# One more pair of FFN tiles by seven products, one pair fewer in the split by token halves

## The chip, the cores and the metric

The kernel runs on one core of a Trainium2 chip. The metric is the device time of one launch in microseconds, as the median of several runs. The engines are TensorE (PE in the profile, with its weight loads as PEld), VectorE (DVE), ScalarE (ACT), GpSimd (POOL) and SyncE (SP, which issues the DMAs). TensorE's clock has two levels, 1.2 and 2.4 GHz; the profile gives the granted clock as a share of the higher.

## The reference, cut to what matters

Two layers (DEPTH = 2) of a hybrid diffusion backbone work on 128 context tokens and 512 latent tokens, D = 1024, FFN width 2816. What the change touches is the FFN of each layer:

```
h = _rmsnorm(x, g_pre_ffn[l]) * (1.0 + sc2) + sh2
y = (jax.nn.silu(h @ w_ffn_gate[l]) * (h @ w_ffn_up[l])) @ w_ffn_down[l]
x = x + gt2 * _rmsnorm(y, g_post_ffn[l])
```

Behind it the next layer begins with a norm and modulation of x and its input projection; after layer 1, x is the output.

## The kernel before, in words

All 640 tokens are worked together, features on the partitions. The tokens lie in two halves of 320 columns (HW): half 0 holds the 128 context tokens and 192 latent ones, half 1 the rest. The input h is eight tiles `hk[k]`, one for 128 features each. Every fp32 operand is split into a high and a low fp32r part, and a product is three passes (high x high, high x low, low x high). A matmul in the profile has 320 columns; one weight tile of 128 output features over all 1024 inputs and one token half takes 8 x 3 = 24 of them.

**The FFN.** Its 22 feature tiles are worked in six groups (`GROUPS` = 4, 3, 3, 4, 4, 4). For each tile there is a pair of weight tiles, gate and up. A group first makes `acts` (silu of gate times up, split again in two parts), and then adds its share of the down projection w_dn to `z`, eight output tiles for each half (`dn`, `ev_dn`).

**Two ways for a pair.** The plain way, `ev_ffn`, runs gate and up for one half: 48 matmuls. The other, `seven`, makes both halves of a pair at once from seven products of half the depth, 7 x 12 = 84 matmuls. It reads sums of h made beforehand (tiles `th`; a sum also takes the place of half 1 of `hk[0..3]`) and sums of the weight tiles, made when the weights are split (a job of kind "sums"; a job "second" splits only the second half of a tile, to `hu`), and needs seven additions on VectorE.

**The last group** has four pairs. Two go by `seven` (`early = gn - 2`). Then the pool for weights is closed and opened anew as stage "c", the lane `second_block` turns half 1 of `hk[0..3]` back into h (tile `tb`), and the other two pairs go by halves: for half 0 gate and up of both pairs, then w_dn for half 0; then, after the flag ("block", l), the same for half 1. When half 0's z is complete, the lane `boundary` carries it on beside half 1's matmuls: the norm over features (`norm_scale`: two matmuls `nps` from the sums of squares `ssqz`, then `rsqrt` on ScalarE and VectorE), eight steps `post` (gated norm plus residual `xl`), in layer 0 a second norm and eight steps `pre` and `modulate`, which write half 0 of the next layer's `hk` (a high part, then a low part). The next layer's first products read half 0. In layer 1 `boundary` only writes the output y. Half 1 goes the same way afterwards.

**What sets the order.** Every engine works its instructions in the order in which they are written out. `drive` writes them: a main generator, `bulk`, gives TensorE's products, lanes such as `boundary` and `second_block` put their steps in between by a clock of estimated costs (`Clock`), and a stream of weights feeds the splits. `vg` and `copy` choose VectorE, POOL or ScalarE by the same clock. Weights come by SP's DMAs into a ring of three raw tiles, in the fixed order of `items`; a split frees its raw tile, and goes to the outer ring (three tiles `hl`, place 0) or to the stage's own pool (place 1). The list `jobs` holds kind, place and stage of every split. The edit stands in the loop that fills `items` and `jobs` (lines 576 to 596), and in the last group (lines 2054 to 2097).

Of the kernel before, what the change touches and what calls it, by code (L numbers as in the profile page):

```python
# [335 lines left out]
def emit(ctx, tc, a, o):  # L336
# [101 lines left out]
    def until(flag):  # L438
        while flag not in flags:
            yield WAIT  # L440

    def room(n):
        while live[0] + n > NSLOT:
            yield WAIT
# [114 lines left out]
    def plain(src, k, n, where, when):  # L559
        items.append((src, k, n))  # L560
        jobs.append(("plain", (len(items) - 1,), 1, where, when))

    for l in range(DEPTH):
        for c, u in [(c, u) for c in ((0, 1, 2) if l == 0 else (0, 2, 1)) + (3, 4, 5, 6, 7) for u in range(2)] + [(9, 0), (8, 0), (8, 1), (9, 1), (10, 0), (10, 1)]:
            k, n = (4, 256) if c in VCH else (KT, 128)
            plain(a["win"][l, c, u].rearrange("p (k n) -> p k n", n=n), k, n, int(l > 0 and (1 <= c <= 2 or (c == 3 and u == 1))), "c")
        for c in range(8):
            plain(a["wout"][l, c], KT, 128, int(c >= 3), "a")
        kb, turns = 0, 0

        def place():
            nonlocal turns
            turns += 1
            return (turns - 1) // 3 % 2

        for gi, gn in enumerate(GROUPS):
            last = gi == len(GROUPS) - 1
            for k in range(gn):
                gu = [(a["wgu"][l, 2 * (kb + k) + i], KT, 128) for i in range(2)]
                if gi and k < gn - 2 * last:  # L580

                    items.extend(gu)
                    g, u = len(items) - 2, len(items) - 1
                    jobs.append(("plain", (g,), 0, place(), "b"))
                    jobs.append(("second", (u,), 0, 2, "b"))
                    jobs.append(("sums", (g, u), 1, place(), "b"))
                    jobs.append(("plain", (u,), 1, place(), "b"))
                else:
                    for i in range(2):
                        plain(*gu[i], int(k == gn - 1) if last else int(2 * k + i >= 3), "c" if last else "a")  # L590
            t = a["wdn"].tensor
            for m in range(0, 8, 2):
                off = l * DFF * D + 128 * kb * D + m * 128 * gn * 128
                src = bass.AP(t, off, [[gn * 128, 128], [128 * gn * 128, 2], [1, gn * 128]])
                plain(src, 2 * gn, 128, int(m < 6) if last else place(), "c" if last else "b")
            kb += gn

    class Stream:
# [93 lines left out]
    stream = Stream()  # L692
# [786 lines left out]
    def bulk():  # L1479
# [117 lines left out]
        for l in range(DEPTH):  # L1597
# [183 lines left out]
            hls = [(nm, m, stream.next()) for nm, m in (("ag", 1), ("rg", 0), ("rg", 1))]  # L1781
# [68 lines left out]
            hls = [stream.next() for _ in range(2)]  # L1850
# [160 lines left out]
            for gi, gn in enumerate(GROUPS):  # L2011
                first_, last = gi == 0, gi == len(GROUPS) - 1
# [25 lines left out]
                if first_:  # L2038

                    hls = []  # L2040
                    for half in range(2):
                        for k in range(gn):
                            if half == 0:
                                hls.append((stream.next(), stream.next()))
                            ps = yield from mm_multi([(hl, half) for hl in hls[k]], hk, hk2key)
                            ev_act(silu(ps[0]), ps[1], acts[k], half)
                            if half:
                                stream.done(*hls[k])
                    flags.add(("first", l))
                    hpool("b", 3)  # L2050
                    mods_in[0] = True
                    yield from room(3)
                    z4 = [u5([128, 2, TOK], "z") for _ in range(3)]
                    zt = lambda k, z4=z4: z4[k // 2][:, k % 2, :]
                else:
                    yield from until(("sums", l))
                    early = gn - 2 if last else gn
                    for k in range(early):
                        yield from seven(acts[k])
                if last:  # L2060
                    if l == 0:
                        yield from until("mods1")
                    hpool("c", 5)
                    free(6)
                    yield from room(2)
                    spawn(second_block(), True)
                    sz = u5([128, 4, HW], "ssqz")
                    ssqs = [[sz[:, i], sz[:, 2 + i]] for i in range(2)]

                    hls = [(stream.next(), stream.next()) for _ in range(2)]  # L2070
                    hds = []
                    for half in range(2):
                        if half:
                            yield from until(("block", l))
                        for k in range(2):
                            yield from ev_ffn(*hls[k], acts[early + k], half)
                            if half:
                                stream.done(*hls[k])
                        if half:
                            lnexp()  # L2080
                        for i in range(4):
                            if not half:
                                hds.append(stream.next())
                            jobs = [(hds[i], 2 * i + m, half) for m in range(2)]
                            if i == 0:
                                yield from dn(jobs)
                            else:
                                for job in jobs:
                                    yield from dn([job])
                            if half:  # L2090
                                stream.done(hds[i])
                        if half == 0:
                            xls = yield from residual(0, xsrc)
                            spawn(boundary(0, zt, ssqs[0], xls, dst, nxt, der[l][:, 3]))
                else:
                    for i in range(4):
                        if len(z4) == i:
                            yield from room(1)
                            z4.append(u5([128, 2, TOK], "z"))
                        hl = stream.next()  # L2100
                        jobs = [(hl, 2 * i + m, half) for m in range(2) for half in range(2)]
                        if i == 0:
                            yield from dn(jobs)
                        else:
                            for job in jobs:
                                yield from dn([job])
                        stream.done(hl)
# [137 lines left out]
```

## Time and profile before

| what | us |
|---|---|
| median of 3 runs (1647.58 to 1650.80) | 1648.89 |
| the profiled execution's own time | 1650.12 |
| its span, first to last instruction | 1648.3 |
| TensorE busy in it | 1591.3 (97%) |
| VectorE busy in it | 1175.3 (71%) |
| ScalarE busy in it | 737.2 (45%) |

The span is what the rows below are timed in, from its start. A row of the timeline is a run of like instructions on one engine; the number in square brackets is the time in which the engine stood idle before it, and behind the arrow what ended that. Every instruction has the line of one helper, so that rows are told apart by their tiles: `acc<-h` are products with h (gate and up, or the next layer's projections), `acc<-act` are w_dn, `nps<-ssqz` is the norm's sum, `hl<-raw` a weight split.

### The profile page before, as it was taken

The numbers are of one execution on the slowest core, as the hardware profiler recorded it, in microseconds if no ns is written. First come the engines' busy times: TensorE is split into PE (matmuls) and PEld (weight loads), VectorE is DVE, ScalarE is ACT, GpSimd is POOL, SyncE is SP. The second block draws the span as 40 slices with busy tenths as digits, with TensorE's granted clock in tenths as the row PEclk, the third lists the DMA queues.
The fourth block names the chain that finished last, engine by engine and source line by source line (L and its number), as shares of the span: only waits on it lengthen the run. The fifth ranks groups of instructions, "written<-read, shape, count | busy, mean of one in ns | idle before, by whom it ended". The sixth has DMA issues, their size and how long they took to land.

```text
span 1648.3 us, 31142 instructions
## 1 busy us (share of the span) xinstructions
PE 1591.3 (97%) x12400; PEld 1479.7 (90%) x12400; DVE 1175.3 (71%) x2346; ACT 737.2 (45%) x1531; POOL 288.7 (18%) x331
## 2 busy tenths in 40 slices
PE   5998999999999999999999999899999999999997
PEld 3887888999999989999999978788999999999996
DVE  6388866758767667676696589777686677767666
ACT  5345654756322323242364466647653333334232
POOL 0101142023100001010143021341231010101012
PEclk9999999999999999999999999899999999999998
DMA  9431332352455655232342211113331213132222
GB/s 379 144 128 51 112 112 72 118 174 96 154 191 184 217 200 183 75 103 65 122 137 90 81 45 55 62 43 121 117 119 60 84 52 105 57 109 93 74 84 96
DMA packets 80002, 188.16 MB, mean 114 GB/s; under 512 B 7633, under 2 KB 38257, under 8 KB 79857
## 3 DMA queue, kind: packets, MB, share of 16 engines
q1 hardware_dynamic: 79856, 186.17, 33.2%
q8 instruction: 98, 1.61, 0.4%
q14 instruction: 48, 0.39, 0.1%
HBM read 173.42 MB, written 12.71 MB: 113 GB/s over the span
## 4 chain that ended last, share of the span: by engine, by line
PE 75%; DVE 13%; ACT 4%; issue 3%; DMA 3%; POOL 1%; SPq 0%; DVEq 0%; POOLq 0%; ACTq 0%
PE acc L235 57%; PE acct L235 6%; PE mps L235 3%; DVE hl L235 2%; DVE gE L235 1%; DMA mraw<-in_wmod 1%; PE rops L235 1%; DVE z L235 1%; DVE qbd L235 1%; DVE sg L235 1%; PE nps L235 1%; DMA raw<-in_wgu 1%; PE nsp L235 1%; DVE raw L235 1%; ACT hl L235 1%
## 5 line engine op out<-in xcount | busy, mean ns | idle before, releaser
L235 PE MATMUL acc<-h,hl 128*128 128x320 f32 x4800 | 758.2, 313 | 5.7 <-DVE h L235 2.0
L235 PEld LDWEIGHTS acc<-h,hl 128*128 128x128 f32 x4800 | 711.2, 188 | 28.7 <-issue 14.9
L235 DVE TENSOR_TENSOR hl<-raw,hl 128x1024 fp32r<-128x1024 f32 (+1 forms) x219 | 264.2, 1213 | 84.6 <-ACT hl L235 84.1
L235 PE MATMUL acc<-act,hl 128*128 128x320 f32 x2112 | 316.7, 310 | 2.2 <-DVE z L235 1.0
L235 PEld LDWEIGHTS acc<-act,hl 128*128 128x128 f32 x2112 | 310.4, 188 | 7.8 <-issue 3.3
L235 ACT ACTIVATE hl<-raw 128x1024 fp32r<-128x1024 f32 (+1 forms) x204 | 206.5, 1034 | 184.3 <-DVE raw L235 93.2
L235 POOL TENSOR_TENSOR raw<-raw 128x512 f32<-128x512 f32 x45 | 59.7, 1327 | 520.6 <-DVE hu L235 469.3
L235 PE MATMUL acct<-hl,h 128*128 128x256 f32 x960 | 137.4, 294 | 2.8 <-DVE hl L235 2.4
L235 PEld LDWEIGHTS acct<-hl,h 128*128 128x128 f32 x960 | 122.2, 193 | 11.4 <-issue 5.9
L235 PE MATMUL acc<-th,hl 128*128 128x320 f32 x768 | 120.0, 310 | 1.3 <-DVE hl L235 0.7
L235 PEld LDWEIGHTS acc<-th,hl 128*128 128x128 f32 x768 | 113.9, 188 | 5.1 <-issue 2.5
L235 ACT ACTIVATE act<-sg 128x320 fp32r<-128x320 f32 x64 | 30.2, 472 | 160.2 <-DVE sg L235 160.2
L235 DVE TENSOR_TENSOR z<-z,acc 128x320 f32<-128x320 f32 x160 | 72.5, 480 | 26.5 <-PE acc L235 26.1
L235 DVE TENSOR_TENSOR act<-sg,act 128x320 fp32r<-128x320 f32 x88 | 50.2, 571 | 35.2 <-ACT act L235 34.4
L235 DVE TENSOR_TENSOR raw<-raw 128x512 f32<-128x512 f32 x83 | 57.2, 689 | 21.7 <-POOL raw L235 20.1
L235 ACT ACTIVATE sg<-sg 128x320 f32<-128x320 f32 x64 | 30.1, 470 | 85.7 <-DVE sg L235 83.6
L235 DVE TENSOR_TENSOR u<-u,acc 128x320 f32<-128x320 f32 x96 | 46.3, 482 | 28.3 <-PE acc L235 27.2
L235 PE MATMUL acc<-th,hu 128*128 128x320 f32 x384 | 62.8, 310 | 0.0
L235 PEld LDWEIGHTS acc<-th,hu 128*128 128x128 f32 x384 | 57.7, 188 | 2.1 <-issue 2.1
L235 PE MATMUL mps<-mraw,ct 128*32 128x256 f32 x768 | 56.3, 399 | 0.2 <-DMA mraw<-in_wmod 0.2
L235 POOL TENSOR_TENSOR h<-xl,h 128x320 fp32r<-128x320 f32 x42 | 38.4, 927 | 84.1 <-DVE h L235 55.0
L235 DVE TENSOR_TENSOR sg<-sg,u 128x320 f32<-128x320 f32 x64 | 34.6, 540 | 19.7 <-ACT sg L235 18.6
(277 smaller groups left out, 1889.0 us busy)
## 6 DMA issues: line engine op xcount, KB each, us to landing
mraw<-in_wmod SPq DMA_DIRECT2D x96, 512.0 KB
raw<-in_wgu SPq DMA_DIRECT2D x88, 512.0 KB
raw<-in_win SPq DMA_DIRECT2D x44, 512.0 KB
raw<-in_wdn SPq DMA_DIRECT2D x32, 512.0 KB
raw<-in_wout SPq DMA_DIRECT2D x16, 512.0 KB
xl<-xd SPq DMA_DIRECT2D x12, 640.0 KB
raw<-in_wdn SPq DMA_DIRECT2D x16, 384.0 KB
xd<-y SPq DMA_DIRECT2D x32, 160.0 KB
```

What stands on the lines that cost most here:

```text
L235: x = fn(*args, **kw)
```

## The change

In each layer the third pair of the last group goes by `seven` too (`early = gn - 1`), so only the fourth goes by halves. The jobs follow: the third pair's are the four jobs of the `seven` way, the fourth pair's gate and up are both split into the outer ring (place 0), and all four w_dn loads of this group into the stage's pool (place 1). The loads and their order are the same.

```diff
--- before.py
+++ after.py
@@ -577,7 +577,7 @@
             last = gi == len(GROUPS) - 1
             for k in range(gn):
                 gu = [(a["wgu"][l, 2 * (kb + k) + i], KT, 128) for i in range(2)]
-                if gi and k < gn - 2 * last:
+                if gi and k < gn - last:
 
                     items.extend(gu)
                     g, u = len(items) - 2, len(items) - 1
@@ -587,12 +587,12 @@
                     jobs.append(("plain", (u,), 1, place(), "b"))
                 else:
                     for i in range(2):
-                        plain(*gu[i], int(k == gn - 1) if last else int(2 * k + i >= 3), "c" if last else "a")
+                        plain(*gu[i], 0 if last else int(2 * k + i >= 3), "c" if last else "a")
             t = a["wdn"].tensor
             for m in range(0, 8, 2):
                 off = l * DFF * D + 128 * kb * D + m * 128 * gn * 128
                 src = bass.AP(t, off, [[gn * 128, 128], [128 * gn * 128, 2], [1, gn * 128]])
-                plain(src, 2 * gn, 128, int(m < 6) if last else place(), "c" if last else "b")
+                plain(src, 2 * gn, 128, int(m < 8) if last else place(), "c" if last else "b")
             kb += gn
 
     class Stream:
@@ -2054,7 +2054,7 @@
                     zt = lambda k, z4=z4: z4[k // 2][:, k % 2, :]
                 else:
                     yield from until(("sums", l))
-                    early = gn - 2 if last else gn
+                    early = gn - 1 if last else gn
                     for k in range(early):
                         yield from seven(acts[k])
                 if last:
@@ -2067,12 +2067,12 @@
                     sz = u5([128, 4, HW], "ssqz")
                     ssqs = [[sz[:, i], sz[:, 2 + i]] for i in range(2)]
 
-                    hls = [(stream.next(), stream.next()) for _ in range(2)]
+                    hls = [(stream.next(), stream.next())]
                     hds = []
                     for half in range(2):
                         if half:
                             yield from until(("block", l))
-                        for k in range(2):
+                        for k in range(1):
                             yield from ev_ffn(*hls[k], acts[early + k], half)
                             if half:
                                 stream.done(*hls[k])
```

The order changes with it. **TensorE, layer 0, from the end of half 0 to the start of half 1** (the `act` products are w_dn, `h_122` to `h_129` the eight tiles of h); before:

```order
L235 MATMUL acc<-act,hl 128x320 x96
L235 MATMUL acc<-h_122,hl 128x320 x3
L235 MATMUL acc<-h_123,hl 128x320 x3
L235 MATMUL acc<-h_124,hl 128x320 x3
L235 MATMUL nps<-ssqz,cst 128x320 x2
L235 MATMUL acc<-h_125,hl 128x320 x3
L235 MATMUL acc<-h_126,hl 128x320 x3
L235 MATMUL acc<-h_127,hl 128x320 x3
```

and now:

```order
L235 MATMUL acc<-act,hl 128x320 x96
L235 MATMUL nps<-ssqz,cst 128x320 x2
L235 MATMUL acc<-h_122,hl 128x320 x3
L235 MATMUL acc<-h_123,hl 128x320 x3
L235 MATMUL acc<-h_124,hl 128x320 x3
L235 MATMUL acc<-h_125,hl 128x320 x3
```

The norm of half 0 stands directly behind its last product; it stood nine matmuls later.

**VectorE, layer 0, about half 0's second norm** (`z` with `acc` is an addition to z for half 1, `r1`, `nps` the norm's two operations, `xl` the first product of `pre`); before:

```order
L235 TENSOR_TENSOR z_5169<-z_5169,acc_9501 128x320
L235 SCALAR_TENSOR_TENSOR r1_9526<-nps_9522,r1_9526 128x320
L235 SCALAR_TENSOR_TENSOR nps_9522<-r1_9526,r0_9525 128x320
L235 TENSOR_TENSOR xl_9317<-z_5169,nps_9522 128x320
L235 TENSOR_TENSOR z_5170<-z_5170,acc_9549 128x320
L235 TENSOR_TENSOR z_5170<-z_5170,acc_9570 128x320
L235 TENSOR_TENSOR z_5171<-z_5171,acc_9587 128x320
L235 TENSOR_SCALAR xl_9317<-xl_9317,der1_83,modt1_82 128x128
L235 TENSOR_TENSOR xl_9317<-z_5169,nps_9522 128x320
```

and now:

```order
L235 TENSOR_TENSOR z_5171<-z_5171,acc_9596 128x320
L235 CAST hl_9633<-raw_9255 128x1024
L235 TENSOR_TENSOR hl_9633<-raw_9255,hl_9633 128x1024
L235 TENSOR_TENSOR z_5442<-z_5442,acc_9616 128x320
L235 TENSOR_TENSOR z_5442<-z_5442,acc_9645 128x320
L235 TENSOR_TENSOR hl_9658<-raw_9270,hl_9658 128x1024
L235 SCALAR_TENSOR_TENSOR r1_9630<-nps_9626,r1_9630 128x320
L235 SCALAR_TENSOR_TENSOR nps_9626<-r1_9630,r0_9629 128x320
L235 TENSOR_TENSOR xl_9383<-z_5169,nps_9626 128x320
L235 TENSOR_SCALAR xl_9383<-xl_9383,der1_83,modt1_82 128x192
L235 TENSOR_TENSOR xl_9383<-z_5169,nps_9626 128x320
```

The norm came behind the second addition to z of half 1; it comes now behind the eighth and a weight split.

**VectorE, layer 1, half 1** (`act` is the evaluation of the pair, `der1` is in a scaling); before:

```order
L235 TENSOR_TENSOR z_14486<-z_14486,xl_17811 128x320
L235 SCALAR_TENSOR_TENSOR z_14486<-z_14486,der1_83,nps_17823 128x128
L235 SCALAR_TENSOR_TENSOR z_14486<-z_14486,der1_83,nps_17823 128x192
L235 TENSOR_TENSOR z_14486<-z_14486,xl_17811 128x320
L235 TENSOR_TENSOR sg_17929<-sg_17929,acc_17931 128x320
L235 CAST act_17283<-sg_17929 128x320
L235 TENSOR_TENSOR act_17283<-sg_17929,act_17283 128x320
L235 TENSOR_TENSOR z_14276<-z_14276,acc_17967 128x320
L235 TENSOR_SCALAR z_14276<-z_14276,der1_83 128x320
L235 TENSOR_TENSOR z_14276<-z_14276,acc_17968 128x320
```

and now:

```order
L235 TENSOR_TENSOR act_17294<-sg_17935,act_17294 128x320
L235 SCALAR_TENSOR_TENSOR z_14289<-z_14289,der1_83,nps_17888 128x128
L235 SCALAR_TENSOR_TENSOR z_14289<-z_14289,der1_83,nps_17888 128x192
L235 TENSOR_TENSOR z_14289<-z_14289,xl_17885 128x320
L235 SCALAR_TENSOR_TENSOR z_14497<-z_14497,der1_83,nps_17888 128x128
L235 SCALAR_TENSOR_TENSOR z_14497<-z_14497,der1_83,nps_17888 128x192
L235 TENSOR_TENSOR z_14497<-z_14497,xl_17885 128x320
L235 SCALAR_TENSOR_TENSOR z_14497<-z_14497,der1_83,nps_17888 128x128
L235 SCALAR_TENSOR_TENSOR z_14497<-z_14497,der1_83,nps_17888 128x192
L235 TENSOR_TENSOR z_14287<-z_14287,acc_17974 128x320
L235 TENSOR_SCALAR z_14287<-z_14287,der1_83 128x320
L235 TENSOR_TENSOR z_14287<-z_14287,acc_17975 128x320
```

Before, the second pair's evaluation stood between the post steps and the first z; now the remaining post steps stand between the one pair's evaluation and z, and the last step's addition of `xl` comes later.

## Rows read from the trace of the kernel before

**Rows 1.** The page, part 1: busy us, share of the span, instructions.

```profile
PE 1591.3 (97%) x12400; PEld 1479.7 (90%) x12400; DVE 1175.3 (71%) x2346; ACT 737.2 (45%) x1531; POOL 288.7 (18%) x331
```

**Rows 2.** Timeline of TensorE, layer 0's last group: start, us, engine, line, work, count, [idle before].

```profile
789.98 16.00 PE L235 MATMUL acc<-h,hl 128*128 128x320 f32 x108
805.82 14.30 PE L235 MATMUL acc<-act,hl 128*128 128x320 f32 x96
819.96 1.48 PE L235 MATMUL acc<-h,hl 128*128 128x320 f32 x9
...
837.75 1.24 PE L235 MATMUL nps<-ssqz,cst 128*128 128x320 f32 x4
838.58 12.02 PE L235 MATMUL acc<-act,hl 128*128 128x320 f32 x78
850.44 0.31 PE L235 MATMUL acc<-h,hl 128*128 128x320 f32 x1
852.70 5.02 PE L235 MATMUL acc<-h,hl 128*128 128x320 f32 x32 [1.95 <-POOL h L235]
```

**Rows 3.** Timeline of VectorE, the same stretch.

```profile
820.16 0.49 DVE L235 TENSOR_TENSOR z<-z,acc 128x320 f32<-128x320 f32 x1 [1.27 <-PE acc L235]
...
831.50 1.06 DVE L235 TENSOR_TENSOR act<-sg,act 128x320 fp32r<-128x320 f32 x1
...
844.02 0.49 DVE L235 SCALAR_TENSOR_TENSOR r<-nps,r 128x320 f32<-128x320 f32 x1 [0.96 <-ACT r L235]
...
845.08 0.49 DVE L235 TENSOR_TENSOR xl<-z,nps 128x320 f32<-128x320 f32 x1
...
854.99 0.35 DVE L235 TENSOR_SCALAR xl<-xl,der,modt 128x128 f32<-128x128 f32 x1
```

**Rows 4.** Timeline of ScalarE, the same stretch.

```profile
820.68 0.47 ACT L235 ACTIVATE ssqz<-z 128x320 f32<-128x320 f32 x1 [1.23 <-DVE z L235]
...
855.59 0.47 ACT L235 ACTIVATE h<-xl 128x320 fp32r<-128x320 f32 x1
```

**Rows 5.** Timeline of POOL, the same stretch.

```profile
851.33 1.32 POOL L235 TENSOR_TENSOR h<-xl,h 128x320 fp32r<-128x320 f32 x1
```

**Rows 6.** Busy us by stretch: five engines (instructions), granted clock, DMA share, GB/s.

```profile
850.00:854.00 4.00, 2.05 (x15) 1.79 (x14) 3.97 (x6) 2.59 (x5) 3.37 (x4) 1.00 0.00 0
974.00:977.00 3.00, 2.66 (x22) 2.29 (x24) 2.52 (x8) 2.04 (x6) 0.00 (x0) 0.50 0.00 0
977.00:980.00 3.00, 3.00 (x39) 2.27 (x37) 1.08 (x5) 1.73 (x6) 0.00 (x0) 0.97 0.03 5
```

**Rows 7.** Timeline of TensorE, layer 1's mixing stage.

```profile
974.34 1.98 PE L235 MATMUL gops<-gat,gv 128*64 128x128 f32 x16 [2.52 <-ACT gat L235]
...
1037.10 0.42 PE L235 MATMUL gdps<-qbd,gE 128*32 128x128 f32 x8 [2.53 <-DVE qbd L235]
```

**Rows 8.** Timeline of TensorE, layer 1's last group.

```profile
1575.46 16.00 PE L235 MATMUL acc<-h,hl 128*128 128x320 f32 x108
...
1605.72 1.48 PE L235 MATMUL acc<-h,hl 128*128 128x320 f32 x9
...
1635.64 1.36 PE L235 MATMUL nps<-ssqz,cst 128*128 128x320 f32 x4 [0.53 <-POOL ssqz L235]
```

**Rows 9.** Timeline of VectorE, half 1 of layer 1's last group.

```profile
1617.23 0.49 DVE L235 TENSOR_TENSOR act<-sg,act 128x320 fp32r<-128x320 f32 x1
...
1620.55 0.49 DVE L235 TENSOR_TENSOR z<-z,xl 128x320 f32<-128x320 f32 x1
...
1630.34 0.48 DVE L235 TENSOR_TENSOR z<-z,acc 128x320 f32<-128x320 f32 x1
...
1631.72 0.48 DVE L235 TENSOR_TENSOR z<-z,acc 128x320 f32<-128x320 f32 x1
...
1635.15 0.49 DVE L235 TENSOR_TENSOR z<-z,acc 128x320 f32<-128x320 f32 x1 [0.29 <-PE acc L235]
```

**Rows 10.** The page, part 5: a weight split on VectorE, count, busy us, mean ns, idle.

```profile
L235 DVE TENSOR_TENSOR hl<-raw,hl 128x1024 fp32r<-128x1024 f32 (+1 forms) x219 | 264.2, 1213 | 84.6 <-ACT hl L235 84.1
```

## The prediction

> **What bounds the kernel now.** I read the page first: TensorE is busy for 97% of the span [rows 1], so the kernel is its instruction stream plus a few places where it waits. Then I read TensorE's timeline through the last FFN group of layer 0 [rows 2] and of layer 1 [rows 8], because the edit works there. The reader is to see three things. One matmul with 320 columns costs TensorE 0.1467 us: 108 of them run from 789.98 to 805.82. In layer 0 the one wait of the stretch is 1.95 us before 852.70, for h, released by POOL: the next layer starts on half 0 before its input is there. In layer 1 nothing waits until the last norm at 1635.64.
>
> So two places decide. At the end of layer 0, half 0 goes through norm, residual, second norm and modulation (on VectorE, ScalarE, POOL) while TensorE computes half 1; this cover is 192 matmuls, 28.2 us, and it is already 2 us too short. At the end of layer 1 the last norm waits for the last z of half 1.
>
> **What the change takes away.** A pair of feature tiles by plain products is 2 tiles x 2 halves x 8 x 3 = 96 matmuls; by seven products of 4 x 3 it is 84. So 12 x 0.1467 = 1.76 us per layer, 3.52 us in all [rows 2]. This is on the path, as TensorE is full there.
>
> **What it adds off TensorE.** The third pair needs seven additions of 0.49 us (the size of the z additions, [rows 3]), one and a half more weight splits of 1.21 us on VectorE [rows 10], and four sums of half a weight tile, three of which POOL takes. That is about 6 us of VectorE per layer, in a stretch whose pairs already run so without a wait; I cost it at nothing. The loads are the same ones: SP issues the same weight tiles in the same order, and the four w_dn tiles come earlier against the gate/up tiles, since these are split into the outer ring before the pool changes. Half 0 has now 144 matmuls before its end instead of 192. VectorE must do in it four w_dn splits and one of the next w_in (5 x 1.21), the conversion of h and the pair's evaluation (some eight operations of 0.3 to 0.8 us), about 11 us by my estimate from these durations, and begins it only behind the third pair's evaluation. The first z is then a few us late, which the rotation of five accumulators covers. Bounds 0 to 1 us, if a load lands late; I take 0.
>
> **What it moves: layer 0.** I count from 791.74, the end of the second pair's seven products (789.98 + 12 x 0.1467).
>
> End of half 0: before 819.96; now 84 + 48 + 96 = 228 matmuls, 33.44 us, so 825.18: +5.22 us. Call the end of half 0 zero from here on.
>
> Half 1 before: the flow of the next layer starts at 852.70, 32.74 us after it [rows 2].
>
> Half 1 after: TensorE's first item is now the norm's matmuls, where before nine of half 1 stood ahead of it. They read ssqz, which ScalarE finishes 1.19 us after the end (820.68 + 0.47 less 819.96, [rows 4]); with the half of the norm's 0.83 us (838.58 less 837.75, [rows 2]) that comes after it, half 1 begins at 1.6. 48 matmuls and the first 18 of w_dn bring TensorE to 11.3. There it reads the pair's act. In VectorE's order this stands behind four and a half of the eight post-norm steps, as the first pair's did before, and ended 12.6 after (831.50 + 1.06, [rows 3]): before nobody waited for it yet, now TensorE loses 1.2 us. All 144 matmuls (21.12), the second norm (0.83) and the wait: half 1 ends at 1.6 + 21.12 + 1.2 + 0.83 = 24.75.
>
> Then h of the next layer. Before, the second norm's VectorE part came after the second z of half 1; now it stands behind the eighth and a weight split. From TensorE's last matmul: 0.20 to the z (820.16 less 819.96), 0.49 z, 1.21 split, 1.06 for the norm's two operations (845.08 less 844.02), 0.49 product, 0.35 scale and shift, 0.47 high part on ScalarE, 1.32 low part on POOL [rows 3 to 5, 10]: 5.6, some overlap, I take 5.5. The flow starts at 30.25. So half 1 gives back only 2.5 us of its 7.04, and layer 0 gets 5.22 - 2.49 = **+2.7 us**. Bounds: +0.7 without the two new waits (0.8 and 1.2), +3.7 if a ScalarE split of about 1 us (beside a row of 1.21 on VectorE) gets between two links.
>
> **The clock.** The wait at the layer's end grows from 2 us to 5.3. After today's wait the granted clock in the stretch 850 to 854 is 1.00 [rows 6]. After the 2.52 us before 974.34 [rows 7] it is 0.50, the lower level of 1.2 GHz, for 3 us and 0.97 in the next 3 [rows 6]. A longer wait is nearer to the second: 0.50 x 3 + 0.03 x 3 = **1.6 us**, bounds 0 (as after 852.70) and 3.2 (two such stretches). The Trainium skill, "TensorE: Matmul & The Clock Gate", "HAM oscillation — how this bites in real kernels", says that a burst of matmuls that follows an idle stretch starts at the halved clock, and that this is paid anew at each stretch; by that rule the change pays where the kernel before did not. The row at 974 agrees, and by the row at 850 alone the sum would be 1.6 us smaller.
>
> **What it moves: layer 1.** The end of half 0 comes 33.44 us after 1577.22 instead of at 1605.72 [rows 8]: +4.94. Half 1 is bound by VectorE afterwards. Post-norm steps and the pair's act end as before at 1620.55, 14.83 after half 0's end, only that the addition at 1620.55 is now put off [rows 9]. From there eight z, each with its scaling behind ScalarE's square, 1.38 us apart when VectorE is behind (1630.34 to 1631.72): 14.83 + 7 x 1.38 + 0.41 for the addition put off = 24.9 for the last z, against 29.43 before (1635.15 less 1605.72). TensorE would allow 1.6 + 21.12 + 0.4 + 0.2 = 23.3 (0.4: act at 1617.72, 12.0 after). So layer 1 gets 4.94 - 4.53 = **+0.4 us**, bounds -1.1 (TensorE's pace) and +0.4. The tail behind the last z is the same.
>
> **Half 1 at the layer's start.** Its second norm now stands ahead of rather than behind a block of five k steps; 0 to 1 us, I take 0.3.
>
> **The sum.** 2.7 + 1.6 + 0.4 + 0.3 = +5.0 us, against the profiled execution's 1650.12: 1655.1. The median of the runs shown is 1.23 lower, 1648.89, so I predict **1653.9**. A step of 0.2% (3.3 us) is about what a measurement of this kernel can tell from no change; the forecast is just past it.
>
> **The rivals.** *The mixing stage takes it up* (1651.4, or 1648.9). In layer 1's mixing TensorE waits 2.52 us at 974.34 and 2.53 at 1037.10 for ScalarE and VectorE [rows 7]. If those chains go by their own work, a TensorE that comes 4 us later waits less, by one such wait (-2.5) or both (-5.0). It decides by whether these chains start from data that TensorE has made late: for it, VectorE's queue is full there; against it, they start from the projections, which follow the late h. Chance, together with a clock that does not fall (1652.3): 0.32.
>
> *The products alone* (1645.4), faster. If h of half 0 is ready when TensorE ends half 1, in layer 0, and the last z keeps TensorE's pace in layer 1, the 3.52 us remain. It decides at the second norm of half 0: h must land within 24.75 of half 0's end. Before, it took 32.7, and the order now puts that norm behind the last z, so it would have to come before its own queue does. Chance 0.08.
>
> *The change does less than it says*: the built order has 84 for 96 matmuls and the moved norms; no chance of its own.
>
> **Chances and range.** Forecast 0.60. The bounds sum to 0.7 + 0 - 1.1 + 0 = -0.4 and 3.7 + 3.2 + 0.4 + 1 + 1 = +9.3, so 1648.5 to 1658.2; the rival's 1648.9 is inside, and I give 1 us below: 1647.5 to 1658. Slower by over 0.2%: 0.60; within: 0.32; faster: 0.08.
>
> **What would show it.** In the profile after: in layer 0, TensorE's wait before the first h matmul of the next layer at about 5 us, released by POOL, and the granted clock at 0.50 right after it; a wait of about 1 us before the norm at half 1's start and another at its w_dn products, for act; the last half 1 of layer 1 with z operations 1.38 apart on VectorE. If the wait at the layer's end stays near 2 us, the chain of 5.5 is wrong, and the time goes to the faster rival; if it is there but the waits of the mixing stage are shorter, the first rival holds.

## The result, and the profile after

The changed kernel takes 1666.24 us (median; 1664.59 to 1671.91) against 1649.41 for the kernel before on the same chip: a ratio of 1.0111, 95% interval 1.0093 to 1.013. The forecast was 1653.9 with a range up to 1658.0; the direction was right, the size was not. The page, part 1 (columns as in [rows 1]), shows the seven products: TensorE has 24 instructions fewer than before and 2.9 us less busy time, and VectorE has more:

```profile
PE 1588.4 (96%) x12376; PEld 1475.4 (89%) x12376; DVE 1190.4 (72%) x2370; ACT 741.0 (45%) x1536; POOL 292.8 (18%) x334
```

So TensorE has less to do, and the rest is waiting. To see where, I cut the span at places that both traces have: (a) the `hu` product of the second pair in layer 0's last group, (b) layer 1's first `lrp` product, (c) the last `rops` product of layer 1's retention, (d) the output projection (the long run of `acc<-h` behind its wait), (e) the first `hu` product of layer 1's FFN, (f) the `hu` product of the second pair in its last group. All in us; e1, e3, e4 and e9 are experiments below.

| stretch | before | after | difference | e1 | e3 | e4 | e9 |
|---|---|---|---|---|---|---|---|
| start to a | 788.22 | 786.34 | -1.88 | 787.82 | 787.96 | 787.51 | 787.98 |
| a to b, end of layer 0 | 79.75 | 84.24 | +4.49 | 81.16 | 85.30 | 80.34 | 79.73 |
| b to c, mixing of layer 1 | 248.31 | 246.11 | -2.20 | 244.44 | 245.36 | 248.70 | 245.13 |
| c to d, end of the mixing | 19.70 | 28.91 | +9.21 | 19.70 | 19.72 | 28.91 | 19.71 |
| d to e | 150.70 | 152.50 | +1.80 | 150.72 | 150.70 | 151.76 | 150.69 |
| e to f, FFN of layer 1 | 287.02 | 288.47 | +1.45 | 287.08 | 287.08 | 289.67 | 287.05 |
| f to the end | 74.60 | 76.13 | +1.53 | 76.78 | 77.08 | 75.71 | 73.71 |
| span | 1648.3 | 1662.7 | +14.4 | 1647.7 | 1653.2 | 1662.6 | 1644.0 |

Each column is one profiled execution, so the spans differ by 14.4 us where the medians differ by 16.8. Small entries need not be effects: the first row ends before any product that the edit changes, and yet scatters from 786.34 to 788.22.

The largest entry is one that the prediction has no term for: 9.21 us at the end of layer 1's mixing, some 250 us behind the end of layer 0, whose last group is the nearest edit. No instruction there was added or taken away. TensorE's timeline before (columns as in [rows 2]; `hmu` and `hps` are the two matmuls that norm a chunk of the retention output `ro`, and `acc<-h` are the last products for the gates `ag` and `rg` and then the first ones of the output projection, whose further products need an h made of `ro`: the row at 1135.98):

```profile
1116.28 0.71 PE L235 MATMUL rops<-rqd,rst 128*128 128x128 f32 x4
...
1122.17 0.70 PE L235 MATMUL hps<-hsq,cst 128*128 128x256 f32 x2 [0.36 <-ACT hsq L235]
...
1124.32 0.70 PE L235 MATMUL hps<-hsq,cst 128*128 128x256 f32 x2 [1.02 <-ACT hsq L235]
1124.67 10.61 PE L235 MATMUL acc<-h,hl 128*128 128x320 f32 x70
1135.98 25.09 PE L235 MATMUL acc<-h,hl 128*128 128x320 f32 x167 [0.70 <-DVE h L235]
```

and after:

```profile
1116.69 0.71 PE L235 MATMUL rops<-rqd,rst 128*128 128x128 f32 x4
...
1121.42 6.95 PE L235 MATMUL acc<-h,hl 128*128 128x320 f32 x45
1128.21 1.02 PE L235 MATMUL hps<-hsq,cst 128*128 128x256 f32 x4
1128.89 6.87 PE L235 MATMUL acc<-h,hl 128*128 128x320 f32 x42
1142.33 0.63 PE L235 MATMUL acc<-h,hl 128*128 128x320 f32 x1 [6.57 <-ACT h L235]
1145.60 26.88 PE L235 MATMUL acc<-h,hl 128*128 128x320 f32 x167 [2.65 <-DVE h L235]
```

These `acc` products are the cover for the norm. Before, the last `hps` stands behind 24 of them, counted from the last `rops`, and 70 run while the rest of the chain goes on; after, it stands behind 63 (45 of them in one run), and the 42 that are left are too few. ScalarE and VectorE add to it: before, the last exponential of the norm and its two squares follow one another at once (the row of three), and the last norm is written to `ro` at 1128.51; after, a table load and two Silu stand between the last exponential and the two squares, and the same write comes at 1136.70:

```profile
1125.57 1.03 ACT L235 ACTIVATE r<-r 128x256 f32<-128x256 f32 x3
1128.51 0.42 DVE L235 SCALAR_TENSOR_TENSOR ro<-ro,hps 128x256 f32<-128x256 f32 x1
```

```profile
1130.16 0.42 ACT L235 ACTIVATE r<-r 128x256 f32<-128x256 f32 x1
...
1130.92 1.28 ACT L235 ACT_TABLE_LOAD   x1
1132.22 0.74 ACT L235 ACTIVATE ag<-ag 128x640 f32<-128x640 f32 x1
1132.86 0.72 ACT L235 ACTIVATE rg<-rg 128x640 f32<-128x640 f32 x1
1133.49 0.71 ACT L235 ACTIVATE r<-r 128x256 f32<-128x256 f32 x2
1136.70 0.42 DVE L235 SCALAR_TENSOR_TENSOR ro<-ro,hps 128x256 f32<-128x256 f32 x1
```

(The first fence is before, the second after.) The waits of 6.57 and 2.65 us stand in place of one of 0.70. Behind them the projection runs at the lower clock; the granted clock is the third number from the end (columns as in [rows 6]):

```profile
1145.00:1148.00 3.00, 2.40 (x9) 2.40 (x10) 2.52 (x5) 1.06 (x2) 0.00 (x0) 0.50 0.80 276
```

### The profile page after: what moved, and what is told of

It reads as the page before. It is cut to its first block, busy times and chain, and to the rows that moved or that the text cites. A ratio compares the mean times of both kernels' runs of the same rounds, so it can differ in the third digit from the quotient of the medians.

```text
span 1662.7 us, 31153 instructions
## 1 busy us (share of the span) xinstructions
PE 1588.4 (96%) x12376; PEld 1475.4 (89%) x12376; DVE 1190.4 (72%) x2370; ACT 741.0 (45%) x1536; POOL 292.8 (18%) x334
## 4 chain that ended last, share of the span: by engine, by line
PE 72%; DVE 16%; ACT 5%; issue 4%; DMA 1%; POOL 1%; DVEq 0%; SPq 0%; ACTq 0%; POOLq 0%
PE acc L235 56%; PE acct L235 5%; PE mps L235 3%; DVE z L235 2%; DVE hl L235 2%; DVE gE L235 2%; DVE qbd L235 1%; PE rops L235 1%; PE nps L235 1%; DVE sg L235 1%; DVE raw L235 1%; ACT r L235 1%; ACT hl L235 1%; DMA raw<-in_wgu 1%; PE nsp L235 1%
## 5 line engine op out<-in xcount | busy, mean ns | idle before, releaser
L235 PE MATMUL acc<-h,hl 128*128 128x320 f32 x4704 | 747.2, 314 | 16.9 <-ACT h L235 11.3
L235 PEld LDWEIGHTS acc<-h,hl 128*128 128x128 f32 x4704 | 699.6, 189 | 40.5 <-issue 14.7
L235 ACT ACTIVATE hl<-raw 128x1024 fp32r<-128x1024 f32 (+1 forms) x208 | 210.5, 1034 | 177.2 <-DVE raw L235 99.4
L235 POOL TENSOR_TENSOR raw<-raw 128x512 f32<-128x512 f32 x49 | 65.2, 1331 | 589.4 <-DVE hu L235 537.3
L235 PE MATMUL acc<-th,hl 128*128 128x320 f32 x816 | 127.4, 311 | 1.3 <-DVE hl L235 0.7
L235 PEld LDWEIGHTS acc<-th,hl 128*128 128x128 f32 x816 | 121.0, 188 | 5.1 <-issue 2.5
L235 PE MATMUL acc<-th,hu 128*128 128x320 f32 x408 | 66.7, 311 | 0.0
L235 PEld LDWEIGHTS acc<-th,hu 128*128 128x128 f32 x408 | 61.3, 188 | 2.1 <-issue 2.1
```

Source lines behind the costliest of these rows:

```text
L235: x = fn(*args, **kw)
```

## Why would an edit of the FFN move a norm of the retention?

By the program, `drive` holds a lane back while the estimated time of VectorE or ScalarE is more than 2.5 us ahead of the present, and takes the present from TensorE's estimated time, which sums up what was written out so far. The edit changes layer 0's end in these estimates, so what is let in at which point shifts for the rest of the program. Theory A: the 9.21 us come from that alone, an accident of the order. Theory B: the seven products cost VectorE or the queues so much that the mixing is late. The first four runs part them.

**e1 and e2, one layer each.** The condition of each edited line gets the layer, for instance

```diff
-                    early = gn - 1 if last else gn
+                    early = gn - (1 if l == 1 else 2) if last else gn
```

for e1, and `l == 0` for e2.

> The change in layer 1 alone; layer 0 as before. Theory A (the time went mainly to layer 1's mixing stage, where the order written out by the clock of estimated costs puts the last norms of the retention later, because layer 0's end was estimated to be earlier; layer 1 itself does not cost much): the order up to layer 1's last group is that of the kernel before, so only the last group differs, +1.5 us (139.72 to 141.25 from its h product to the end), up to +3 with the wait found one group earlier. About 1651, ratio 1.001 to 1.002. Theory B (the seven products themselves press on VectorE, in both layers alike): about half of the +16.8, so 1657 or more.

> The change in layer 0 alone; layer 1's last group as before. Here the order of layer 1's mixing has the late norms, as in the changed kernel. Theory A: +3.25 (layer 0's end) -1.57 (start of layer 1) +9.82 (end of the mixing) +1.8 (the products behind its wait, at a lower clock) = +13.3, about 1662 to 1663. Theory B: half of +16.8, about 1658.

Measured: e1 1649.59 us, ratio 1.0005 (0.9996 to 1.0015); e2 1666.82, ratio 1.0115 (1.0099 to 1.013). In layer 1 the change is worth nothing that the medians show (by the interval, 0.7 us less to 2.5 more), and layer 0's alone costs all of it, some 4 us more than A expected and 9 more than B.

**e3 and e4, the order moved with no change of work.** Only a number of the planner's clock is changed at layer 0's end; 4000 ns on the changed kernel (e3), 8000 on the kernel before (e4):

```diff
             xsrc = dst
             pctx = fctx
+            if l == 0:
+                clock.t["PE"] += 4000.0
```

> The changed kernel; 4000 ns are added to the estimated time of TensorE at layer 0's end, a number that only the writing-out of the order reads. No work is changed. By this the norms of layer 1's retention stand as in the kernel before (24 filler products ahead of the last one instead of 63). Theory A: TensorE's two waits of 6.57 and 2.65 us before the output projection shrink to the one of 0.7 of the kernel before, and the slow stretch behind them goes: 9.8 + 1.8 = 11.6 less than the changed kernel, about 1654.6; layer 0's +3.25 and layer 1's +1.5 stay. Theory B (the waits come from the work or the traffic of the seven products, not from the order): they stay, about 1666.

> The kernel before, with 8000 ns added at the same place to the estimated time of TensorE. No work is changed, and the last group keeps its two pairs by halves. By this the norms of layer 1's retention stand as late as in the changed kernel (63 filler products ahead of the last). Theory A: +9.8 + 1.8 = +11.6, about 1661, with TensorE waiting some 9 us before the output projection. Theory B: no wait there, within 2 us of 1649.4.

Measured: e3 1654.05 us, ratio 1.0032 (1.0019 to 1.0045), 0.55 from A's number; e4 1664.82, ratio 1.0097 (1.0082 to 1.0112), 4 us above A's. The stretch from c to d is 19.72 and 28.91. e3's rows, and then e4's:

```profile
1126.66 0.70 PE L235 MATMUL hps<-hsq,cst 128*128 128x256 f32 x2 [1.02 <-ACT hsq L235]
1127.01 10.61 PE L235 MATMUL acc<-h,hl 128*128 128x320 f32 x70
1138.34 25.08 PE L235 MATMUL acc<-h,hl 128*128 128x320 f32 x167 [0.71 <-DVE h L235]
```

```profile
1128.07 1.02 PE L235 MATMUL hps<-hsq,cst 128*128 128x256 f32 x4
1128.74 6.86 PE L235 MATMUL acc<-h,hl 128*128 128x320 f32 x42
1142.19 0.63 PE L235 MATMUL acc<-h,hl 128*128 128x320 f32 x1 [6.59 <-ACT h L235]
1145.46 26.15 PE L235 MATMUL acc<-h,hl 128*128 128x320 f32 x167 [2.65 <-DVE h L235]
```

The wait comes and goes with the order, in either kernel, and is there in e4 without the edit. Theory A is shown, B falls. e4's surplus over 11.6 lies partly in layer 1's FFN (e to f, +2.65), where the new order has a further wait of 1.72 us, for VectorE.

**e5, the same by another handle.** The norm lane is put at the head of the lanes, which the hold-back does not apply to:

```diff
-                    spawn(norm(c))
+                    spawn(norm(c), True)
```

> The changed kernel; the lane that norms a chunk of the retention is put at the head of the lanes, where a backlog of VectorE and ScalarE does not hold it back. It sets the place of the norms by itself, and not over an estimate of the time: the last of them stand 36 filler products behind the last retention product, in place of 63 in the changed kernel and 24 in the kernel before. Theory A (o of the retention is late because its norms are put late): 12 fillers more than in the kernel before are 12 x 0.1467 = 1.8 us, so TensorE waits 0.7 + 1.8 = 2.5 us before the output projection in place of 9.2, and the slow stretch of 1.8 us behind it goes mostly: 7 to 8.5 us less than the changed kernel, 1658 to 1659. Theory B (the nudge of the first experiments did it in another way): above 1662.

Measured: 1659.40 us, ratio 1.0068 (1.0053 to 1.0083), 6.8 under the changed kernel, a little past A's number. From c to d it takes 19.78, as in the good order, with waits of 0.15 and 2.23 us. By medians e5 is 5.35 us above e3, and most of that stays open. Some 1.2 us of it stand behind the wait of 2.23 (d to e takes 151.91 against 150.70). In its trace b to c takes 249.33 against 245.36, but that is no price of putting the norms first: e6, e7 and e8 below do the same and take 243.75, 243.87 and 244.97 there. So the place of the norms is the cause, and this is not the cure.

**e6 and e7, layer 0's own price.** e3 is still 4.5 us above e1; that is layer 0's last group. The prediction put it down to the place of half 0's second norm in VectorE's queue. e6 puts the lane that holds it first, on top of e5, and e7 does both in the kernel before:

```diff
-                            spawn(boundary(0, zt, ssqs[0], xls, dst, nxt, der[l][:, 3]))
+                            spawn(boundary(0, zt, ssqs[0], xls, dst, nxt, der[l][:, 3]), l == 0)
```

> As e5, and in layer 0 half 0's lane of norm, residual, second norm and modulation at the head of the lanes too. The second norm's matmuls then stand behind 21 of the 96 w_dn products of half 1; they stood behind 81. Theory A (layer 0 loses because half 0's second norm is queued behind half 1's z): TensorE's wait of 4.6 + 0.5 us at the layer's end shrinks to under 1.5 us and the granted clock stays at 1.00, so 3 to 5 us less than e5, about 1654. Theory B (VectorE has more work in half 1 than its 21 us, whatever the order): the wait moves to act and z within half 1, within 1 us of e5.

> The kernel before with both of these orders (norms of the retention first, half 0's lane first in layer 0); no change in the products. It tells what the third pair by seven products is worth where the order is the same. The wait of 1.95 us at layer 0's end should go, the one before the output projection grows from 0.7 to 2.5 us: within 2 us of 1649.4. Against it the seven products should save up to 1.76 us in layer 0 if e6 has no wait left there, and cost about nothing in layer 1, so e6 would be at most 2 us under e7; if e6 is slower than e7, half 1's 21 us in layer 0 are too short in any order.

Measured: e6 1664.08 us, ratio 1.0095 (1.0078 to 1.0112), 4.7 worse than e5; e7 1656.74, ratio 1.005 (1.0035 to 1.0065), some 7 above its number. Putting half 0's lane first is bad in either kernel: a to b takes 89.39 in e7, against 79.75 in the kernel before, and 93.76 in e6, against 84.47 in e5. And e6 is 7.3 slower than e7, 4.4 of it from a to b: with this order in both kernels, the shorter half 1 costs the changed one as much as e3 against e1. The second norm does come 60 matmuls earlier in e6, and TensorE waits elsewhere, for act, z and a weight split:

```profile
840.84 1.43 PE L235 MATMUL acc<-act,hl 128*128 128x320 f32 x3 [3.99 <-DVE act L235]
...
859.03 1.36 PE L235 MATMUL acc<-h,hl 128*128 128x320 f32 x5 [2.49 <-DVE z L235]
861.69 0.64 PE L235 MATMUL acc<-h,hl 128*128 128x320 f32 x1 [1.30 <-DVE hl L235]
864.21 2.50 PE L235 MATMUL nps<-ssqz,cst 128*128 128x320 f32 x4 [1.89 <-POOL ssqz L235]
```

So an earlier place in the queue is not enough. The third busy time of a row is VectorE's; first the kernel before, from half 0's end to the next layer's products, then e3:

```profile
819.96:852.70 32.74, 30.79 (x203) 29.67 (x202) 26.20 (x53) 20.03 (x35) 14.25 (x15) 1.00 0.38 133
```

```profile
825.00:855.37 30.37, 25.69 (x157) 23.28 (x157) 27.81 (x56) 18.87 (x34) 11.37 (x12) 0.99 0.35 122
```

VectorE has 26 to 28 us of work in this stretch. In the kernel before TensorE's 192 matmuls (28.2 us) covered it; 144 (21.1 us) do not, and VectorE is busy 92% of the time. In e6 and e7 the lane's new place changes who waits, and does not shorten the waits.

**e11 and e12, less work for VectorE there.** e11 forces the weight splits of this half onto ScalarE and POOL, e12 leaves out half 0's residual additions; both with the good order of the norms (by 8000 and 5000 ns).

```diff
                         if half:
                             yield from until(("block", l))
+                            bias[0] = (-1e5, -1e5)
```

```diff
             y = normed(k)
             yield
-            vg(y, y, xl(k), ALU.add)
+            if half or not nxt or nxt[1]:
+                vg(y, y, xl(k), ALU.add)
```

> The changed kernel with the order of the norms as in the kernel before (8000 ns added to TensorE's estimated time at layer 0's end), and in layer 0's half 1 the weight splits that are not urgent forced onto ScalarE (high part) and POOL (low part), off VectorE. It is to be compared with e3 (1654.05). Theory A (VectorE has 27.8 us of work in the 30.4 us between half 0's end and the first product of the next layer, and that is what TensorE waits for): some 4 us of splits less on VectorE, so the waits of 2.96 and 1.11 us at the layer's end shrink to 1 us or less, 2 to 4 us less than e3, 1650 to 1652. Theory B (POOL takes 2.5 us for one split, and the sums of squares of the norms and the low parts of h stand behind them on POOL): the wait stays or grows, 1654 or more.

> The changed kernel with the order of the norms as in the kernel before (5000 ns added at the same place), and work left out: the eight additions of the residual xl to z for half 0 in layer 0, most of them on VectorE at 0.40 to 0.49 us. It is to be compared with e3 (1654.05). Theory A (layer 0's loss is VectorE's work in half 1, which TensorE's 21 us no longer cover): 3 us less work, so the wait at the layer's end (4.07 us in e3) goes to about 1 us and the clock stays up: 3 to 4.5 us less than e3, 1649.5 to 1651. Theory B (a fixed chain of norm, high part and low part sets the wait, whatever VectorE's load): within 1 us of e3.

Measured: e11 1657.34 us, ratio 1.0051 (1.0038 to 1.0065), 3.3 worse than e3. Its B holds: POOL becomes the late one.

```profile
853.58 2.50 PE L235 MATMUL nps<-ssqz,cst 128*128 128x320 f32 x4 [4.82 <-POOL ssqz L235]
...
863.76 12.21 PE L235 MATMUL acc<-h,hl 128*128 128x320 f32 x71 [3.03 <-POOL h L235]
```

e12: 1654.31 us, ratio 1.0031 (1.0018 to 1.0044), no less than e3, which A did not expect. At the place itself it goes as A says: with 3 us of VectorE's work gone the wait before h shrinks from 4.07 to nothing, with 1.61 us left before a norm, and a to b takes 79.32 us in place of 85.30. But the order moved with it: the second norm's matmuls stand behind 45 of the w_dn products in e12, and behind 81 in e3. And TensorE then meets the next thing that is late, accumulators that ScalarE has not emptied yet (`gqk`):

```profile
832.03 7.50 PE L235 MATMUL acc<-act,hl 128*128 128x320 f32 x45
839.37 1.24 PE L235 MATMUL nps<-ssqz,cst 128*128 128x320 f32 x4
...
849.70 1.34 PE L235 MATMUL nps<-ssqz,cst 128*128 128x320 f32 x4 [1.61 <-POOL ssqz L235]
...
870.98 0.62 PE L235 MATMUL acct<-hl,h 128*128 128x256 f32 x3 [3.19 <-ACT gqk L235]
```

and b to c takes 250.44 in place of 245.36. What of these 5 us is that wait (3.19) and what the order and the clock, one run does not tell. So the wait at the layer's end is shown to go when VectorE has less work and the norm stands earlier, and an earlier place alone (e6) does not do it. Less work at the same place was not tested cleanly: e11 moved it to POOL, which then was late, and the additions that e12 leaves out are themselves links of the chain that TensorE waits for. That VectorE's load is the cause is argued from its 92%, not shown, and that less of it would shorten the kernel is not shown either.

**e8, e9 and e10, layer 1's end.** There the saved products are lost to z steps on VectorE. In half 1 a z is added, squared on ScalarE and then scaled on VectorE; e8 (on top of e6), e9 (on top of e1) and e10 (on the kernel before) put the scaling on ScalarE:

```diff
-                            copy(zz, zz, BIAS_CP, scale=sc)
+                            S.activation(out=zz, in_=zz, func=AF.Copy, scale=sc)
```

> As e6, and in layer 1's half 1 the scaling of z is put on ScalarE in place of VectorE. Theory A (layer 1's last half goes by VectorE's z additions, 1.38 us apart, since each scaling waits for ScalarE's square): the additions follow TensorE's products, 1.76 us apart at the end, and the last norm begins some 2.2 us earlier; 2 us less than e6, and layer 1 gains instead of costing nothing. Theory B (ScalarE's square and scaling take VectorE's place, or the end is bound by the write of y): within 0.5 us of e6.

> The change in layer 1 alone, as e1, with the scaling of z in layer 1's half 1 on ScalarE. Layer 0 and layer 1's mixing keep the order of the kernel before. Theory A (in layer 1 the saved products are lost to VectorE's z steps of 1.38 us, and e8 took these away): e1's 1649.6 less the 2.4 us by which e8 was under e6, so 1647.2 and a ratio of about 0.9987 to the kernel before. Theory B (e8's gain came from a place of its own order): no different from e1, 1649.5.

> The kernel before with the scaling of z in layer 1's half 1 on ScalarE, and nothing else. Theory A: there TensorE's w_dn products begin later against VectorE's post-norm steps, and the last norm waits 0.53 us; only that can be gained, so 0 to 0.6 us less than the kernel before, ratio 0.9997 to 1. Theory B (VectorE's z steps cost the kernel before as much): 2 us less, and then e9 owes its gain to the scaling alone and not to the seven products.

Measured: e8 1661.62 us, ratio 1.0083 (1.0068 to 1.0098), 2.5 under e6; e9 1647.07, ratio 0.9989 (0.998 to 0.9998); e10 1648.36, ratio 1.0 (0.9991 to 1.0008). VectorE in e1, with the scaling, and then in e9, without:

```profile
1627.33 0.48 DVE L235 TENSOR_TENSOR z<-z,acc 128x320 f32<-128x320 f32 x1
1628.41 0.39 DVE L235 TENSOR_SCALAR z<-z,der 128x320 f32<-128x320 f32 x1 [0.60 <-ACT sq L235]
1628.71 0.48 DVE L235 TENSOR_TENSOR z<-z,acc 128x320 f32<-128x320 f32 x1
```

```profile
1627.29 0.49 DVE L235 TENSOR_TENSOR z<-z,acc 128x320 f32<-128x320 f32 x1 [1.27 <-PE acc L235]
1629.05 0.49 DVE L235 TENSOR_TENSOR z<-z,acc 128x320 f32<-128x320 f32 x1 [1.27 <-PE acc L235]
1630.81 0.49 DVE L235 TENSOR_TENSOR z<-z,acc 128x320 f32<-128x320 f32 x1 [1.27 <-PE acc L235]
```

In e1 a z comes every 1.38 us because the scaling waits 0.60 for the square, and VectorE, which begins late, is still catching up at the end. In e9 it has caught up and waits for TensorE, 1.76 us (12 products) apart. The last stretch falls from 76.78 to 73.71 us; in the kernel before it takes 74.60. The scaling alone (e10) gives nothing, the seven products alone (e1) give nothing, both together give 1.5 us of 1648.6. That is 0.1%: the interval ends just below 1, and e9 is 1.3 us under e10 on the same chip. So e9, the change in layer 1 alone with this scaling, is the one version here that its interval puts below the kernel before.

## Why the prediction was wrong, point by point

**The step that failed** is the sum's silence on what lies between the two last groups. I priced the edit where it stands, and treated layer 1's mixing as given: the only words on it are the rival "the mixing stage takes it up", at -2.5 or -5.0 us. That let the stage's start move, but not its order, although the kernel's words on `drive` say that all later order hangs on the estimates. It was +9.21 us there, with +1.80 behind it at the lower clock (c to e), and e3 takes both away. These 11.0 us are nearly all of the 11.8 by which the measured +16.8 exceeds the +5.0 of the sum. With the order held, the whole sum comes out: e3's 1654.05 against 1653.9. Such closeness is partly luck, since errors cancel: in e3's trace act cost less than its term, the last stretch took 2.48 us more than before, and b to c 2.95 less.

**The rival of the mixing stage** did not happen as put. The two waits that it named are unchanged ([rows 7] has 2.52 and 2.53; after, 2.51 at 978.60 and 2.52 at 1040.70). The 2.20 us less from b to c are no saving: e1 and e9 have the order of the kernel before there and take 3.9 and 3.2 less than it as well, with a granted clock of 0.99 over the stretch against 0.97.

**Layer 0** came out at the size forecast. The flow was forecast 30.25 us after half 0's end; after, half 0's w_dn products end at 823.46, and the two h products that wait begin 29.66 and 30.61 later. Half 1 begins 1.49 after the end (forecast 1.6), its last product ends 25.06 after (24.75), and the wait, 4.60 and 0.50 us, has about the length forecast, though most of it is for h's high part from ScalarE and not for POOL:

```profile
809.22 14.24 PE L235 MATMUL acc<-act,hl 128*128 128x320 f32 x96
823.85 1.50 PE L235 MATMUL nps<-ssqz,cst 128*128 128x320 f32 x4 [0.39 <-POOL ssqz L235]
...
835.36 9.88 PE L235 MATMUL acc<-act,hl 128*128 128x320 f32 x63 [0.29 <-DVE act L235]
...
845.92 2.60 PE L235 MATMUL acc<-act,hl 128*128 128x320 f32 x15
853.12 0.44 PE L235 MATMUL acc<-h,hl 128*128 128x320 f32 x1 [4.60 <-ACT h L235]
854.07 0.90 PE L235 MATMUL acc<-h,hl 128*128 128x320 f32 x2 [0.50 <-POOL h L235]
```

Act cost 0.29 us and not 1.2. The stretch a to b, which holds the terms 2.7, 1.6 and 0.3, measured +4.49; by medians e3 less e1 is 4.5. The reading behind it was too narrow: it has only the norm's place in the queue, but an earlier place alone does not help (e6), and VectorE's 26 to 28 us of work are the likely rest (e12).

**The clock** fell to its lower level after the wait, as forecast:

```profile
853.50:856.50 3.00, 2.50 (x8) 1.85 (x7) 2.96 (x7) 1.77 (x5) 0.51 (x1) 0.50 0.66 247
```

In these 3 us it cost at most 3 x 0.50 = 1.5 us (TensorE is busy in 2.50 of them), near the 1.6 of the term. But a single row was no ground for it: in e1, with layer 0 as before, the clock fell after the unchanged wait too, as the last section shows. So this term was right in part by luck.

**Layer 1** was +1.53 and not +0.4. Half 0's end and the z steps came as forecast, except that two of VectorE's instructions took 1.10 and 1.15 us in place of 0.39 and 0.49 while POOL worked beside them, so the last z began at 1649.56, 25.87 after half 0's end and not 24.9. The first of the two stood in the trace of the kernel before as well (a scaling of 1.10 us at 1626.56), and the sum passed over it. By medians the layer's change costs 0.15 us (e1), inside the bounds given; by the traces the last stretch is 1.5 to 2.5 us longer than before (after, e1, e3), outside them. e1's interval of 0.7 us less to 2.5 more holds both, so this term stays open. The rival of the products alone needed this pace of TensorE here, which only e8 and e9 reach, and an h in time in layer 0, which only e12 had, with work left out.

## What to carry to other kernels

Where a planner with a clock of estimates writes out the order, an edit has two prices: its own, and that of a new order everywhere behind it. The second is read from the built order, not from the trace: compare the order of both kernels to the end, and look at the places where one engine's filler runs out. To part the two on the chip, shift the planner's clock by a number and leave the work alone. And taking work from the engine that hides a chain pays only as far as that chain's engines have time to spare: here, as far as the runs tell, VectorE, 80% busy from half 0's end to the next layer's products under a cover of 28.2 us, had too little left for one of 21.1.

## What the hardware showed that I had not expected

The same wait does not always lower the clock. The same `gops` products follow a wait of 2.52 to 2.54 us for ScalarE in the kernel before [rows 7], e9 and e3. Before, the next 3 us were granted 0.50 and the 3 after them 0.97 [rows 6]. In e9 the drop came again, about 1 us later behind the wait; in e3 there was none (a number between 0.50 and 1.00 is the mean of a stretch in which the clock changed level). e9, then e3:

```profile
975.00:978.00 3.00, 3.00 (x32) 1.79 (x29) 1.85 (x8) 2.04 (x5) 0.00 (x0) 0.54 0.02 5
```

```profile
979.00:982.00 3.00, 2.67 (x44) 2.05 (x45) 2.74 (x10) 2.85 (x8) 0.00 (x0) 1.00 0.00 0
982.00:985.00 3.00, 3.00 (x34) 2.57 (x33) 1.43 (x7) 2.17 (x9) 0.00 (x0) 1.00 0.03 5
```

At layer 0's end it is the same. Behind the wait of 1.95 us the kernel before has 1.00 [rows 6], and its 32 products take 5.02 us [rows 2]. In e1, whose order is the same there, the wait is 1.94, the clock falls, and the same 32 products take 1.46 us more, which is all of e1's surplus from a to b (1.41):

```profile
852.25 6.48 PE L235 MATMUL acc<-h,hl 128*128 128x320 f32 x32 [1.94 <-POOL h L235]
```

```profile
853.00:856.00 3.00, 3.00 (x15) 3.00 (x14) 2.93 (x7) 1.90 (x5) 2.21 (x3) 0.57 0.53 172
```

So the drop is not decided by the wait's length alone, and a stage's time in one profile scatters by some us: from b to c TensorE is busy 236.64 us in the kernel before and 232.20 in e9, with the same 2070 instructions. After the 9.2 us of waiting in the changed kernel and in e4 the clock fell both times. The Trainium skill, "TensorE: Matmul & The Clock Gate", section "HAM oscillation — how this bites in real kernels", describes a kernel in which every burst of matmuls behind a wait for DMA starts at the halved clock, because the wait is long enough to bring it on. The two long waits agree with that. The waits of 1.94 to 2.54 us are shorter than those; there the rows go either way, so they neither bear the section out nor speak against it. The prediction counted the row at 974 as agreeing; with its 2.52 us it is one of these, and e3 shows that it could have gone the other way.

VectorE and POOL hold each other up. In layer 1's last half of the changed kernel a scaling of z, mostly 0.39 us, took 1.10 beside one of POOL's additions to `ssqz`:

```profile
1640.57 1.10 DVE L235 TENSOR_SCALAR z<-z,der 128x320 f32<-128x320 f32 x1 [0.60 <-ACT sq L235]
```

```profile
1640.61 0.88 POOL L235 TENSOR_TENSOR ssqz<-ssqz,sq 128x320 f32<-128x320 f32 x1 [5.87 <-ACT sq L235]
```

It ends 0.18 us after POOL's. In the next five such pairs, where POOL starts 0.11 us behind, the scaling takes 0.39 and POOL's addition 0.99 to 1.02 in place of 0.88. The Trainium skill, "SBUF — State Buffer", section "SBUF: two separate sides", says that GpSimd and certain VectorE instructions (those in a performance mode that uses two ports, or with two inputs in SBUF) share one pair of ports, and that the one which starts first holds it to its end while the other waits. The rows of the five pairs agree with that in direction. In the first, VectorE's instruction is listed 0.04 us ahead and is still the one that is held up, so which was first at the ports they do not show.
